# A two-layer fp32 encoder: output projection of the scan mixer requested one block ahead, a mask scaling moved from VectorE to ScalarE, and a shorter Newton step

## The chip, the cores and the metric

The kernel runs on one core of a Trainium2 chip. The metric is device time in microseconds (us) for one launch, median of three runs. The engines of a core each have their own instruction queue and run in order: TensorE (PE, with its weight loads PEld), VectorE (DVE), ScalarE (ACT), GpSimd (POOL), and SyncE (SP), which here issues the DMA transfers.

## The reference, cut to what matters

```
x: (1, 512, 1024) float32
layer 0:  h = rms_norm(x) @ w_in
          (A) neighbourhood attention, 8 heads of 64
          (B) Mamba-2 scan, 16 heads in 4 groups, 4 chunks of 128 tokens, forward and backward:
              y_diag = sum_s cb[l,s] * exp(a_cum[l] - a_cum[s]) (s <= l) * dt[s] x[s]
              y_off  = C . state . exp(a_cum);  gated by silu(z), group RMS norm
          x = x + concat(A, B) @ w_out          # "output projection", 1536 -> 1024
          x = x + swiglu_ffn(x)
layer 1:  GQA attention with QK norm and axial rotary; x = x + ctx @ w_out;  x = x + swiglu_ffn(x)
```

Every matrix product is fp32-accurate. The kernel splits each operand into a high part `h` and a low part `l` and makes three matmuls of each product (`l.h`, `h.l`, `h.h`).

## The kernel before, in words

All activations lie transposed: eight tiles `res[k]` of 128 channels by 512 tokens. A weight block of 1024 columns is loaded by `load_w` (L139 to L156): one DMA brings the raw block (tag `wr`, two buffers), ACT copies it to the high part (L147, tag `wh`, three buffers), DVE subtracts to get the low part (L149, tag `wl`, three buffers). Eight `mm3` calls, 24 matmuls 512 columns wide, use it. `stream(blocks, ahead)` (L166) takes a list of pairs (a function that loads, a generator that makes the matmuls) and calls the load of block n+1 before the matmuls of block n.

The mixer of layer 0 uses such a stream as filler. The generator `fill` yields after each `mm3`; `run(n)` takes n steps of it between the pieces of the attention and of the scan. PE's order is fixed by hand there (`manual_schedule` for PE); the order on DVE, ACT, POOL and SP is made by a planner, which goes by the order in which the instructions are written and by when it believes their inputs to be ready. The filler has 64 steps of query and key blocks, 192 steps of the scan's input blocks (four groups of six blocks of eight), and then the output projection, `out_blocks` (L696), which stands outside the stream: each of its blocks requests its weights and then at once makes its matmuls. It takes the eight output tiles in three trios; in each trio there are three blocks `oA` of eight steps on the first eight input tiles, and then one block `wq` of six (four in the last trio) on the two tiles of scan group 2. Group 3's two tiles come last, in `tail`.

The last input block of group 3 ends at step 256. The scan of group g starts at step 64 + 48(g+1) + LEAD[g] and takes 10, 8, 10, 2 and 12 steps of filler between its pieces; that of group 2 starts after step 220, so step 256 falls into its last 12 steps, six of which are then steps of the first `oA` block. Behind these stand, on PE, the matmuls `yd` (L650) and `yo` (L663) of group 2's second pair of heads, and then the transposes `bt` (L560) with which group 3 begins. They read the tile `grp` of group 3, on which ACT makes one silu (L542), with a load of its function table ahead of it. The silu needs the convolution of the last input block: one ACT instruction (L522) and three on DVE (L525).

For each of the 16 scan heads, lanes with tag `n` (eight buffers, 128x512) hold `m` (the masked `cb` times `dt`), `cf` and `cb` (two broadcast rows, by DMA), and for heads of a group's second pair (`i == 1`) also `mb`. The forward half of `m` is made by ACT in four chunks (L632). The backward half is added by DVE in four chunks (L634) for the first pair, and by one POOL instruction (L626) and one DVE addition (L641) for the second. The decay `cf` goes through ACT (L636), DVE or POOL (L638, L628, L643), an Exp on ACT (L644) and a product with `m` on DVE (L645), which PE needs for `yd`.

An inverse root is refined by one Newton step: three DVE operations on 128x512 (L205 to L207, L1042 to L1044; 16 times in all) or on a few columns (L214 to L216).

Layer 1 begins with `odd_mixer`. Two key blocks, `kpa` and `kpb`, are made by `project` (L173), and the sum of squares of `res` is made by seven POOL additions (L191) on squares from ACT, while the last blocks of the feed-forward before it are still running. In this mixer the planner orders PE too.

Of the kernel before, what the change touches and what calls it, by code (L numbers as in the profile page):

```python
# [11 lines left out]
AF = mybir.ActivationFunctionType  # L12
ALU = mybir.AluOpType
# [4 lines left out]
P = 128  # L18
# [54 lines left out]
def encoder_kernel(ctx: ExitStack, tc: tile.TileContext, xt, vec, cst, rope, nab, w_v, w_qk, w_dt, w_ssd,  # L73
# [98 lines left out]

    def project(ps, src, xg, name, eng=None):  # L173
        w = load_w(src, 1024, name, eng)
        for k in range(KB):
            mm3(ps, w, k * P, xg[k], ALL, k == 0, k == KB - 1)

# [16 lines left out]
    def rsqrt_wide(ps, inv, name):  # L194
        m = slot(f"{name}_m")
        A.activation(m, ps, AF.Identity, scale=inv, bias=epst)
        return rsqrt_tile(m, name)

    def rsqrt_tile(m, name):
        r = slot(f"{name}_r")  # L200
        t = slot(f"{name}_t")
        A.activation(r, m, AF.Ln)
        A.activation(r, r, AF.Exp, scale=-0.5)
        A.activation(t, r, AF.Square)
        V.tensor_tensor(t, t, m, ALU.mult)  # L205
        V.tensor_scalar(t, t, -0.5, 1.5, ALU.mult, ALU.add)
        V.tensor_tensor(r, r, t, ALU.mult)  # L207
        return r

    def rsqrt_small(m, r, t):  # L210
        A.activation(r, m, AF.Ln)
        A.activation(r, r, AF.Exp, scale=-0.5)
        V.tensor_tensor(t, r, r, ALU.mult)
        V.tensor_tensor(t, t, m, ALU.mult)  # L214
        V.tensor_scalar(t, t, -0.5, 1.5, ALU.mult, ALU.add)
        V.tensor_tensor(r, r, t, ALU.mult)  # L216

# [7 lines left out]
    def even_mixer(lp):  # L225
# [330 lines left out]
        def ssd_group(g, gt):  # L556
# [52 lines left out]
            for i in range(2):  # L609
                yd = bank(f"yd{g}_{i}", "c")  # L610
                es = []
                for hh in range(2):
# [8 lines left out]
                    def per_chunk(t):  # L621
                        return t[:, :, 16 + h:17 + h].to_broadcast([P, NCH, P])

                    if mm:
                        mb = lane(f"mb{h}", "n", 8)
                        G.tensor_tensor(c4(mb), c4(cbg), per_chunk(d3v(dt)), ALU.mult)  # L626
                    if em:
                        G.tensor_tensor(c4(cbk), c4(cbk), per_chunk(d3v(cum)), ALU.subtract)  # L628
                    for c in range(NCH):
                        cc = slice(c * P, (c + 1) * P)  # L630
                        jf, jb = c * 32 + h, c * 32 + 16 + h
                        A.activation(m[:, cc], cbl[:, cc], AF.Copy, scale=dt[:, jf:jf + 1])  # L632
                        if not mm:
                            V.scalar_tensor_tensor(m[:, cc], cbg[:, cc], dt[:, jb:jb + 1], m[:, cc],  # L634
                                                   ALU.mult, ALU.add)
                        A.activation(e[:, cc], cf[:, cc], AF.Identity, bias=ncum[:, jf:jf + 1])  # L636
                        if not em:
                            V.scalar_tensor_tensor(e[:, cc], cbk[:, cc], cum[:, jb:jb + 1], e[:, cc],  # L638
                                                   ALU.subtract, ALU.min)
                    if mm:  # L640
                        V.tensor_tensor(m, m, mb, ALU.add)  # L641
                    if em:
# [53 lines left out]
        def out_blocks():  # L696
            for trio in (range(3), range(3, 6), range(6, KB)):
                ps = {}
                for o in trio:
                    ps[o] = bank(f"oA{o}")  # L700
                    w = load_w(w_o0[o, :, 0:8 * P], 8 * P, f"wo{o}", V)
                    for k in range(8):
                        mm3(ps[o], w, k * P, (ctx_n + ssd_out)[k], ALL, k == 0, False)
                        yield
                w = load_w([w_o0[o, :, 8 * P:10 * P] for o in trio], 256 * len(trio), f"wq{trio[0]}", V)
                for n, o in enumerate(trio):
                    res[o] = xslot(f"xr{o}")
                    nc.sync.dma_start(res[o], xt[o])
                    for k in range(2):
                        mm3(ps[o], w, (2 * n + k) * P, ssd_out[4 + k], ALL, False, k == 1)  # L710
                        yield
                    V.tensor_tensor(res[o], res[o], ps[o], ALU.add)

        blocks = [t for b in range(4) for t in qk_blocks(b)] + [t for g in range(SSD_G) for t in ssd_blocks(g)]

        def both():
            yield from stream(blocks, 1)
            yield from out_blocks()

        fill = both()  # L720
        steps, later = [0], []

# [57 lines left out]
    def ffn(layer, gname, hp):  # L780
# [232 lines left out]
        with tc.manual_schedule(engines={mybir.EngineType.PE, mybir.EngineType.DVE, mybir.EngineType.Activation}):  # L1013
# [19 lines left out]
            def norm():  # L1033
                ps = bank(f"{name}_ss", "c")
                T.matmul(ps, ones_r, ql, start=True, stop=False)
                T.matmul(ps, ones_r, qh, start=False, stop=True)
                m, r, t = (slot(f"{name}_{n}") for n in "mrt")
                A.activation(m, ps, AF.Identity, scale=1.0 / D, bias=epst)
                A.activation(r, m, AF.Ln)
                A.activation(r, r, AF.Exp, scale=-0.5)  # L1040
                A.activation(t, r, AF.Square)
                V.tensor_tensor(t, t, m, ALU.mult)  # L1042
                V.tensor_scalar(t, t, -0.5, 1.5, ALU.mult, ALU.add)
                V.tensor_tensor(r, r, t, ALU.mult)  # L1044
                rstd.append(r)
# [77 lines left out]
    def odd_mixer(op):  # L1123
# [39 lines left out]
        pa, pb = bank("kpa"), bank("kpb")  # L1163
        project(pa, w_kv[0], xg, "wka")
        project(pb, w_kv[1], xg, "wkb")
        acc = sumsq("o")
        ksq = [slot(f"oksq{n}") for n in range(2)]
# [358 lines left out]
```

## Time and profile before

| | us |
|---|---|
| three runs | 1288.01, 1289.76, 1290.24 |
| median | 1289.76 |
| the profiled execution: its time | 1290.49 |
| its span, first to last instruction | 1288.7 |
| around the span | 1.8 |
| mean granted TensorE clock | 0.995 |

The profile is of one execution, 0.73 us above the median of the three runs. Times inside it are counted from the span's start. The layers lie in it so: attention and scan of layer 0 from 0 to about 350, feed-forward to about 718, layer 1's attention to about 925, feed-forward to the end. An instruction's row gives its start and its duration; a figure in square brackets is how long its engine stood idle before it and what released it.

### The profile page before, as it was taken

What the parts mean: (1) busy time and instruction counts of PE and PEld (TensorE: products, weight loads), DVE (VectorE), ACT (ScalarE), POOL (GpSimd) and SP (SyncE); (2) the same over time, 40 slices, a digit from 0 to 9 for tenths busy, and PEclk for the clock granted to TensorE, in tenths of its full rate; (3) what the DMA queues carried; (4) which work ended last, traced back from release to release, by engine and by line L of the source; (5) the groups of instructions that cost most, each with busy time, mean ns of one, the idle gap of its engine ahead of it and who ended that gap; (6) DMA issues with size and microseconds to landing.
All of it is one profiled execution on the core that took longest, in us unless ns stands there. A gap on an engine that the chain in (4) does not pass through costs nothing.

```text
span 1288.7 us, 20006 instructions
## 1 busy us (share of the span) xinstructions
PE 1264.0 (98%) x7502; PEld 1101.0 (85%) x7502; DVE 1000.4 (78%) x1688; ACT 716.1 (56%) x1335; POOL 166.4 (13%) x184
## 2 busy tenths in 40 slices
PE   9999999989999999999999999999999999999998
PEld 8777788867888899989998778778888899889987
DVE  6788798997789898738953668998889998549732
ACT  6676568766455456514643547777565455325521
POOL 5022111011100000000002334655100000000000
PEclk9999999999999999999999999999999999999999
DMA  7334343545333333332223443321223333423132
GB/s 235 107 99 148 112 138 123 164 120 166 123 116 113 99 99 114 117 98 84 91 78 96 144 97 101 83 66 34 83 82 98 106 107 104 123 79 105 54 117 92
DMA packets 52081, 139.03 MB, mean 108 GB/s; under 512 B 6992, under 2 KB 8144, under 8 KB 51984
## 3 DMA queue, kind: packets, MB, share of 16 engines
q1 hardware_dynamic: 51696, 137.23, 34.7%
q8 instruction: 59, 0.97, 0.3%
q10 hardware_dynamic: 288, 0.52, 0.1%
q14 instruction: 38, 0.31, 0.1%
HBM read 127.11 MB, written 2.23 MB: 100 GB/s over the span
## 4 chain that ended last, share of the span: by engine, by line
PE 70%; DVE 17%; ACT 6%; issue 4%; DMA 2%; SPq 0%; POOL 0%; ACTq 0%; DVEq 0%; POOLq 0%
PE fo L160 5%; PE fo L162 5%; PE fo L161 5%; PE fa L162 5%; PE fa L161 5%; PE fa L160 5%; PE fb L161 3%; PE fb L160 3%; PE fb L162 3%; PE vps L278 2%; PE opt L1281 1%; PE fc L162 1%; PE fc L161 1%; PE fc L160 1%; PE fg L1009 1%
## 5 line engine op out<-in xcount | busy, mean ns | idle before, releaser
L147 ACT ACTIVATE wf_h<-wf_r 128x1024 fp32r<-128x1024 f32 (+1 forms) x76 | 69.5, 919 | 125.8 <-PE fo L162 68.3
L160 PE MATMUL fo<-hh,wf_l 128*128 128x512 f32 x352 | 137.2, 390 | 1.2 <-DVE wf_l L149 1.2
L161 PE MATMUL fo<-hl,wf_h 128*128 128x512 f32 x352 | 137.0, 389 | 0.0
L162 PE MATMUL fo<-hh,wf_h 128*128 128x512 f32 x352 | 136.9, 389 | 0.0
L984 DVE TENSOR_TENSOR xr<-xr,fo 128x512 f32<-128x512 f32 x48 | 32.2, 685 | 113.6 <-PE fo L162 113.6
L149 DVE TENSOR_TENSOR wf_l<-wf_r,wf_h 128x1024 fp32r<-128x1024 f32 (+1 forms) x76 | 78.8, 1053 | 15.0 <-ACT wf_h L147 15.0
L160 PEld LDWEIGHTS fo<-hh,wf_l 128*128 128x128 f32 x352 | 66.1, 188 | 15.5 <-DVE wf_l L149 2.0
L162 PEld LDWEIGHTS fo<-hh,wf_h 128*128 128x128 f32 x352 | 66.1, 188 | 13.8
L161 PEld LDWEIGHTS fo<-hl,wf_h 128*128 128x128 f32 x352 | 66.1, 188 | 13.6
L160 PE MATMUL g<-n_xh,w_l 128*128 128x512 f32 x192 | 76.6, 399 | 0.0
L162 PE MATMUL g<-n_xh,w_h 128*128 128x512 f32 x192 | 75.3, 392 | 0.0
L161 PE MATMUL g<-n_xl,w_h 128*128 128x512 f32 x192 | 75.2, 392 | 0.0
L910 ACT ACTIVATE sl<-sb 128x256 f32<-128x256 f32 x34 | 14.3, 419 | 90.7 <-DVE sb L909 90.7
L191 POOL TENSOR_TENSOR o_acc<-o_acc,o_sq 128x512 f32<-128x512 f32 x7 | 12.3, 1753 | 383.2 <-ACT o_sq L190 383.2
L1272 POOL TENSOR_SCALAR op<-op,osum 128x512 f32<-128x512 f32 x64 | 45.4, 718 | 55.5 <-DVE osum L1271 38.6
L1270 ACT ACTIVATE op<-os,omx 128x512 f32<-128x512 f32 x64 | 43.6, 686 | 15.1 <-DVE omx L1268 12.9
L1285 DVE TENSOR_TENSOR opt<-opt,opt 128x512 fp32r<-128x512 f32 x64 | 43.5, 683 | 7.2 <-ACT opt L1284 6.5
L1284 ACT ACTIVATE opt<-opt 128x512 fp32r<-128x512 f32 x64 | 37.9, 598 | 18.7 <-PE opt L1281 18.1
L791 ACT ACTIVATE sa<-fa 128x256 f32<-128x256 f32 x68 | 25.4, 374 | 36.3 <-PE fa L162 36.3
L1268 DVE TENSOR_REDUCE omx<-os 128x1 f32<-128x512 f32 x64 | 42.0, 679 | 4.5 <-PE os L1266 4.4
L791 ACT ACTIVATE gh<-gr 128x1024 fp32r<-128x1024 f32 x34 | 35.6, 1047 | 14.0 <-PE fo L162 11.6
L162 PEld LDWEIGHTS g<-n_xh,w_h 128*128 128x128 f32 x192 | 36.1, 188 | 7.5
(2644 smaller groups left out, 4363.9 us busy)
## 6 DMA issues: line engine op xcount, KB each, us to landing
ur<-in_w_fa SPq DMA_DIRECT2D x34, 512.0 KB, 3.6
gr<-in_w_fa SPq DMA_DIRECT2D x34, 512.0 KB, 3.5
w_r<-in_w_ssd SPq DMA_DIRECT2D x24, 512.0 KB, 3.7
wf_r<-in_w_fa SPq DMA_DIRECT2D x20, 512.0 KB, 3.6
wf_r<-in_w_fb SPq DMA_DIRECT2D x32, 320.0 KB, 3.0
wf_r<-in_w_fb SPq DMA_DIRECT2D x16, 512.0 KB, 3.5
wo_r<-in_w_o SPq DMA_DIRECT2D x14, 512.0 KB, 3.8
nb<-in_nab SPq DMA_DIRECT2D x16, 256.0 KB, 3.0
```

The source lines that it names most:

```text
L147: A.activation(hi[:, 0:cols], raw, AF.Copy)
L149: (eng or V).tensor_tensor(lo[:, 0:cols], raw, f(hi)[:, 0:cols], ALU.subtract)
L160: T.matmul(ps, wl[:, a], xh[:, b], start=first, stop=False, skip_group_check=skip)
L161: T.matmul(ps, wh[:, a], xl[:, b], start=False, stop=False, skip_group_check=skip)
L162: T.matmul(ps, wh[:, a], xh[:, b], start=False, stop=last, skip_group_check=skip)
L791: A.activation(dst, src, AF.Copy, scale=scale)
L984: V.tensor_tensor(res[o], res[o], self.banks[o], ALU.add)
L1268: V.tensor_reduce(mx, sps, AX.X, ALU.max, negate=True)
L1270: A.activation(p_, sps, AF.Exp, bias=mx, accum_out=sums)
L1272: G.tensor_scalar(p_, p_, sums, 1.0, ALU.mult, ALU.mult)
L1284: A.activation(hl[:, 0:S], pt, AF.Copy)
L1285: V.tensor_tensor(hl[:, S:2 * S], pt, f(hl[:, 0:S]), ALU.subtract)
```

## The change

- `out_blocks` becomes a list of pairs like the others and is appended to `blocks`, so the stream requests each of its weight blocks one block ahead; `both` goes away. The order of the matmuls stays.
- For heads of a group's first pair, the backward half of the mask is scaled by four ACT copies into a lane `mb` of its own, and one DVE addition (that of the second pair) joins the halves. Four DVE operations per head go away.
- `newton` does the step in two `scalar_tensor_tensor` operations: t = (t * -0.5) * m, r = (t + 1.5) * r.
- `project` gets an order for `kpa` in which the eight matmuls with the low part of the activations come last.
- The sum of squares of layer 1's attention is added on DVE (`V`) and no longer on POOL.

```
-    def project(ps, src, xg, name, eng=None):
-        w = load_w(src, 1024, name, eng)
-        for k in range(KB):
-            mm3(ps, w, k * P, xg[k], ALL, k == 0, k == KB - 1)
+    def project(ps, src, xg, name, late=False):
+        wh, wl = load_w(src, 1024, name)
+        order = [(k, p) for k in range(KB) for p in range(3)]
+        if late:
+            order = [(k, p) for k in range(KB) for p in (0, 2)] + [(k, 1) for k in range(KB)]
+        for m, (k, p) in enumerate(order):
+            T.matmul(ps, (wl if p == 0 else wh)[:, k * P:k * P + P], xg[k][p == 1], start=m == 0, stop=m == 23)
...
+    def newton(r, t, m):
+        V.scalar_tensor_tensor(t, t, -0.5, m, ALU.mult, ALU.mult)
+        V.scalar_tensor_tensor(r, t, 1.5, r, ALU.add, ALU.mult)
...
-        V.tensor_tensor(t, t, m, ALU.mult)
-        V.tensor_scalar(t, t, -0.5, 1.5, ALU.mult, ALU.add)
-        V.tensor_tensor(r, r, t, ALU.mult)
+        newton(r, t, m)
...
+                    mb = lane(f"mb{h}", "n", 8)
                     if mm:
-                        mb = lane(f"mb{h}", "n", 8)
                         G.tensor_tensor(c4(mb), c4(cbg), per_chunk(d3v(dt)), ALU.mult)
...
                         A.activation(m[:, cc], cbl[:, cc], AF.Copy, scale=dt[:, jf:jf + 1])
                         if not mm:
-                            V.scalar_tensor_tensor(m[:, cc], cbg[:, cc], dt[:, jb:jb + 1], m[:, cc],
-                                                   ALU.mult, ALU.add)
+                            A.activation(mb[:, cc], cbg[:, cc], AF.Copy, scale=dt[:, jb:jb + 1])
...
-                    if mm:
-                        V.tensor_tensor(m, m, mb, ALU.add)
+                    V.tensor_tensor(m, m, mb, ALU.add)
...
         def out_blocks():
-            for trio in (range(3), range(3, 6), range(6, KB)):
-                ps = {}
-                for o in trio:
+            ps = {}
+
+            def first(o):
+                def matmuls(w):
                     ps[o] = bank(f"oA{o}")
-                    w = load_w(w_o0[o, :, 0:8 * P], 8 * P, f"wo{o}", V)
                     for k in range(8):
                         mm3(ps[o], w, k * P, (ctx_n + ssd_out)[k], ALL, k == 0, False)
                         yield
...
+                return (lambda: load_w(w_o0[o, :, 0:8 * P], 8 * P, f"wo{o}", V)), matmuls
...
+            for trio in (range(3), range(3, 6), range(6, KB)):
+                for o in trio:
+                    yield first(o)
+                yield rest(trio)
...
-        def both():
-            yield from stream(blocks, 1)
-            yield from out_blocks()
-
-        fill = both()
+        blocks += out_blocks()
+        fill = stream(blocks, 1)
...
-        project(pa, w_kv[0], xg, "wka")
+        project(pa, w_kv[0], xg, "wka", True)
         project(pb, w_kv[1], xg, "wkb")
-        acc = sumsq("o")
+        acc = sumsq("o", V)
```

## Rows read from the trace of the kernel before

**Rows 1.** The page's list of engines: busy us, share of the span, number of instructions.

```profile
PE 1264.0 (98%) x7502; PEld 1101.0 (85%) x7502; DVE 1000.4 (78%) x1688; ACT 716.1 (56%) x1335; POOL 166.4 (13%) x184
```

**Rows 2.** Busy time by stretch of 40 us: the scan of group 2, the stretch in which the output projection begins, and one of layer 1's attention. Columns: stretch, its length, then busy us (instructions) of PE, PEld, DVE, ACT and POOL, granted clock, DMA share, GB/s.

```profile
240.00:280.00 40.00, 39.20 (x226) 32.68 (x225) 37.81 (x66) 31.36 (x60) 4.46 (x4) 1.00 0.42 130
280.00:320.00 40.00, 33.57 (x168) 26.49 (x167) 31.70 (x56) 26.44 (x49) 3.63 (x2) 0.91 0.52 162
840.00:880.00 40.00, 37.51 (x215) 31.25 (x214) 37.11 (x71) 28.87 (x62) 21.52 (x22) 0.96 0.20 54
```

**Rows 3.** The waits of PE over the whole span, longest in total first: who waited, for what, us in total, times, longest.

```profile
PE oA L160 <- ACT cf L636: 4.6, 1, 4.6
...
PE oq_ss L1185 <- DVE oqsq L1235: 1.3, 1, 1.3
...
PE yd L650 <- DVE cf L645: 1.1, 2, 0.8
...
PE oA L160 <- ACT so_xh L180: 0.6, 1, 0.6
PE oA L161 <- DVE so_xl L181: 0.6, 2, 0.3
...
PE kpa L161 <- DVE o_xl L181: 0.5, 1, 0.5
```

**Rows 4.** PE in order of time, from the last matmul of the last scan input block to the first transpose of group 3.

```profile
280.93 0.39 PE L162 MATMUL g<-n_xh,w_h 128*128 128x512 f32 x1
285.91 0.76 PE L160 MATMUL oA<-nch,wo_l 128*128 128x512 f32 x1 [4.60 <-ACT cf L636]
...
292.92 1.09 PE L650 MATMUL yd<-cf,xtok 128*64 128x128 f32 x16
...
295.62 0.63 PE L560 MATMUL bt<-cstt,grp 128*128 128x128 f32 x4
```

**Rows 5.** Busy time of PE in the idle stretch and in the stretch behind it. Columns: stretch, length, PE busy (matmuls), granted clock, DMA share, GB/s.

```profile
281.40:285.90 4.50, 0.00 (x0) 0.89 0.59 117
285.90:291.90 6.00, 5.99 (x14) 0.51 0.51 154
```

**Rows 6.** DVE in order of time over the same place.

```profile
283.89 0.74 DVE L525 SCALAR_TENSOR_TENSOR grp<-g,vect,grp 128x510 f32<-128x510 f32 x1
284.55 1.21 DVE L149 TENSOR_TENSOR wo_l<-wo_r,wo_h 128x1024 fp32r<-128x1024 f32 x1
285.69 0.68 DVE L645 TENSOR_TENSOR cf<-cf,m 128x512 f32<-128x512 f32 x1
286.29 0.74 DVE L525 SCALAR_TENSOR_TENSOR grp<-g,vect,grp 128x511 f32<-128x511 f32 x1
286.95 1.21 DVE L149 TENSOR_TENSOR wo_l<-wo_r,wo_h 128x1024 fp32r<-128x1024 f32 x1
288.08 0.74 DVE L525 SCALAR_TENSOR_TENSOR grp<-g,vect,grp 128x511 f32<-128x511 f32 x1
```

**Rows 7.** ACT in order of time over the same place and the 15 us ahead of it.

```profile
267.35 1.05 ACT L147 ACTIVATE wo_h<-wo_r 128x1024 fp32r<-128x1024 f32 x1
269.44 1.28 ACT L632 ACTIVATE m<-cbl,dt 128x128 f32<-128x128 f32 x4 [1.03 <-DVE cf L645]
...
276.73 1.04 ACT L147 ACTIVATE wo_h<-wo_r 128x1024 fp32r<-128x1024 f32 x1
281.36 0.78 ACT L522 ACTIVATE grp<-g,vect 128x512 f32<-128x512 f32 x1 [3.58 <-PE g L162]
...
288.90 1.28 ACT L542 ACT_TABLE_LOAD   x1 [3.03 <-DVE grp L525]
290.19 2.77 ACT L542 ACTIVATE grp<-grp 128x3072 f32<-128x3072 f32 x1
```

**Rows 8.** ACT in order of time just ahead of the first `wq` block of the output projection.

```profile
313.48 0.41 ACT L636 ACTIVATE cf<-cf,ncum 128x128 f32<-128x128 f32 x1 [2.86 <-DMA cf<-cumd]
...
314.38 0.71 ACT L180 ACTIVATE so_xh<-yn,vect 128x512 fp32r<-128x512 f32 x1
```

**Rows 9.** Groups of instructions by line and operation over the whole span: line, engine, operation, output from inputs, shapes, count, then busy us, mean ns of one, and idle us before them with what ended it.

```profile
L632 ACT ACTIVATE m<-cbl,dt 128x128 f32<-128x128 f32 x64 | 22.7, 393 | 2.7 <-DVE cf L645 1.5 <-DVE cbl L577 1.2
L636 ACT ACTIVATE cf<-cf,ncum 128x128 f32<-128x128 f32 x64 | 22.2, 392 | 12.4 <-DMA cf<-cumd 12.4
L634 DVE SCALAR_TENSOR_TENSOR m<-cbg,dt,m 128x128 f32<-128x128 f32 x32 | 11.0, 395 | 0.0
L641 DVE TENSOR_TENSOR m<-m,mb 128x512 f32<-128x512 f32 x8 | 5.8, 740 | 0.0
L205 DVE TENSOR_TENSOR kn_t<-kn_t,kn_m 128x512 f32<-128x512 f32 x4 | 2.8, 690 | 1.8 <-ACT kn_t L204 1.8
L206 DVE TENSOR_SCALAR kn_t<-kn_t 128x512 f32<-128x512 f32 x4 | 1.7, 419 | 0.0
L181 DVE SCALAR_TENSOR_TENSOR f_xl<-xr,vect,f_xh 128x512 fp32r<-128x512 f32 x16 | 11.1, 745 | 0.0
L191 POOL TENSOR_TENSOR o_acc<-o_acc,o_sq 128x512 f32<-128x512 f32 x7 | 12.3, 1753 | 383.2 <-ACT o_sq L190 383.2
```

**Rows 10.** DVE in order of time while `kpa` is made.

```profile
721.23 2.44 DVE L181 SCALAR_TENSOR_TENSOR o_xl<-xr,vect,o_xh 128x512 fp32r<-128x512 f32 x2
```

More of the change, by code (lines that the diff above doesn't have):

```diff
@@ L213, in rsqrt_small @@
         V.tensor_tensor(t, r, r, ALU.mult)
-        V.tensor_tensor(t, t, m, ALU.mult)
-        V.tensor_scalar(t, t, -0.5, 1.5, ALU.mult, ALU.add)
-        V.tensor_tensor(r, r, t, ALU.mult)
+        newton(r, t, m)
     def bcast_rstd(acc, name):
@@ L704, in out_blocks, with rest, matmuls @@
                         yield
[L705 to L712, printed above, removed]
+                return (lambda: load_w(w_o0[o, :, 0:8 * P], 8 * P, f"wo{o}", V)), matmuls
+            def rest(trio):
+                def matmuls(w):
+                    for n, o in enumerate(trio):
+                        res[o] = xslot(f"xr{o}")
+                        nc.sync.dma_start(res[o], xt[o])
+                        for k in range(2):
+                            mm3(ps[o], w, (2 * n + k) * P, ssd_out[4 + k], ALL, False, k == 1)
+                            yield
+                        V.tensor_tensor(res[o], res[o], ps[o], ALU.add)
+                return (lambda: load_w([w_o0[o, :, 8 * P:10 * P] for o in trio], 256 * len(trio),
+                                       f"wq{trio[0]}", V)), matmuls
+            for trio in (range(3), range(3, 6), range(6, KB)):
+                for o in trio:
+                    yield first(o)
+                yield rest(trio)
         blocks = [t for b in range(4) for t in qk_blocks(b)] + [t for g in range(SSD_G) for t in ssd_blocks(g)]
-        def both():
-            yield from stream(blocks, 1)
-            yield from out_blocks()
-        fill = both()
+        blocks += out_blocks()
+        fill = stream(blocks, 1)
         steps, later = [0], []
@@ L1041, in norm @@
                 A.activation(t, r, AF.Square)
-                V.tensor_tensor(t, t, m, ALU.mult)
-                V.tensor_scalar(t, t, -0.5, 1.5, ALU.mult, ALU.add)
-                V.tensor_tensor(r, r, t, ALU.mult)
+                newton(r, t, m)
                 rstd.append(r)
```

## The prediction, made before the change was run

> **What bounds the kernel now.** I read the list of engines first, then the stretches of 40 us, then PE's waits, and last the order of time on PE, DVE and ACT at the one large wait. The list shows PE busy for 98% of the span [rows 1]: no change to the other engines can be worth more than the time in which PE waits or runs slowly, and the reader should look for that time only. The change takes no matmul away. The stretches show where such time lies: 40 us pass with PE busy for 33.6 and a mean granted clock of 0.91 where the output projection begins, and in the scan ahead of it PE is full while DVE is busy for 37.8 of 40 and ACT for 31.4; layer 1's attention loses some 2.5 us in a like stretch [rows 2]. PE's waits name the largest, 4.6 us ahead of the first `oA` matmul [rows 3].
>
> The order of time tells what that wait is. The profile puts it down to ACT `cf`, whose data these matmuls do not read. What they read are the weights: the high part was copied at 276.7 at the latest, in fact both copies of `wo` then made were over by 277.8 [rows 7], but DVE made the low part only from 284.55 to 285.76, and PE began at 285.91 [rows 4, 6]. So the data lay ready for 7 us or more, and the low part stood behind other work on DVE, because the load is written late in the program. The idle time has a second price: in the 6.0 us behind it the granted clock was 0.51, that is the level of 1.2 GHz [rows 5]. At full clock that work would have taken 6.0 x 0.51 = 3.1, so 2.9 us are lost. The last matmul ahead started at 280.93 and PE was free some 0.25 later, at 281.2; the first `oA` came at 285.91, 4.7 us later. The place costs 4.7 + 2.9 = 7.6 us.
>
> **The change part by part.**
>
> *One block ahead.* The load of the first `oA` block is now written ahead of the last input block of group 3, before the elementwise work of group 2's second pair of heads, so DVE should make its low part before 281.2. Then the 18 matmuls ahead of `yd` follow at once: 285.91 to 292.92 less the 2.9 lost is 4.1 us. `yd` and `yo` take 295.62 - 292.92 = 2.7 [rows 4]. PE would stand before `bt` at 281.2 + 4.1 + 2.7 = 288.0, where it came at 295.62 before.
>
> But `bt` reads the silu of group 3, which ended at 290.19 + 2.77 = 292.96 [rows 7]. This is what is late next. Its chain starts when PE ends the last input block: ACT at 281.36, three DVE operations at 283.89, 286.29 and 288.08, the table load at 288.90, the silu. Between the three stand two weight parts of 1.21 [rows 6]. One of them, the first `wo`, leaves this place; the next starts 285.69 - 284.55 = 1.14 us later than it could, so the silu ends at about 291.8 if the rest keeps its order. PE then waits 291.8 - 288.0 = 3.8 us at `bt`. The gain up to `bt` is 295.6 - 291.9 = 3.7 us. If the clock falls behind this wait as it fell behind the one of 4.6, another 2.9 are lost and 0.8 stays; if not, 3.7. The best end is a chain without foreign work on DVE: 281.36 + 0.78 + 3 x 0.74 + 1.28 + 2.77 = 288.4 [rows 6, 7], and 7.2 us gained. Between 0.8 and 3.7 I take 2.2, as no row shows which way a wait between the two goes. DVE's 1.2 us for the low part do not vanish; they fall earlier, where DVE is full [rows 2], and are covered as long as `yd` finds `cf` ready: it did at 286.4, when L645 ended [rows 6], and PE would come at 285.3. Up to 1.1 us of wait at `yd` is therefore inside the 3.8, not on top of it.
>
> *The wait for `so`.* Further on, the first `wq` block waits for group 2's output, `so`: 0.6 + 0.6 = 1.2 us [rows 3]. ACT made `so_xh` at 314.38, behind a `cf` instruction that had waited 2.86 for its DMA [rows 8]. With group 3 running some us earlier on all engines, DMA and norm move against each other. Bounds: 0 and 1.2; I take 0.6.
>
> *Second mask scaling on ACT.* DVE loses 32 chunk operations, 11.0 us busy, and gains eight additions, 5.8; ACT gains 32 copies like those of L632, 1.28 for four, 10.2 us in all [rows 7, 9]. Over four groups that is -1.3 us of DVE and +2.6 us of ACT in a stretch of about 40, against 37.8 and 31.4 busy [rows 2]: ACT comes to 34 and stays below DVE. What is hidden: the ACT copies run ahead of `cf`, in ACT's idle time (12.4 us of it before `cf`, waiting for DMA [rows 9]). What may show: PE's two waits at `yd` for DVE, 1.1 us in total [rows 3]; the addition is shorter than the chunks were. Bounds: +1.1 gained, and a loss if the copies delay Exp; I take 0.5 gained. If the cover were gone, 10.2 us of ACT would stand in the chain to `yd`.
>
> The Trainium skill (ScalarE: Activation LUTs, Rules for kernel authors) says that additions and multiplications belong on VectorE and not on ScalarE, which speaks against this edit. The trace does not bear it out for this shape: the copy took 393 ns on ACT and the fused operation 395 ns on DVE [rows 9]. By the rule the edit would cost more on ACT than DVE saves; by the rows the two are equal per chunk, and only the load of the engines decides.
>
> *Newton.* Three operations, 0.690 + 0.419 + 0.690 = 1.80, become two of the kind that took 0.745, 1.49 [rows 9]: 0.31 x 16 = 5.0 us of DVE. Most lie under matmuls: around the norms of the feed-forward PE does not wait [rows 3]. Five of the sixteen are in layer 1's attention, where PE loses time to DVE [rows 2, 3]: at most 5 x 0.31 = 1.6 us. I take 0.3. The small forms save one operation each and show nowhere.
>
> *Low part last, and the sum on DVE.* `kpa` waited 0.5 us for `o_xl`, in a stretch where two such operations took 2.44 instead of 2 x 0.745 [rows 3, 9, 10]. With 16 matmuls ahead of the first low part, the wait goes: 0.5 gained (bounds 0 and 0.5). The seven additions, 12.3 us on POOL, become 7 x 0.690 = 4.8 on DVE [rows 9], five or six of them under the last feed-forward blocks, where DVE has idle time; they cost nothing while that lasts, and 0.7 each if one falls between the last `o_xl`.
>
> *Sum:* 2.2 + 0.6 + 0.5 + 0.3 + 0.5 = 4.1 us. The profiled execution would go from 1290.49 to 1286.4; it lay 0.7 above the median, so against 1289.76 I forecast **1285.6**. All best ends give 7.2 + 1.2 + 1.1 + 1.6 + 0.5 = 11.6, or 1278.2; the bounds without a new mechanism end at 1289.0 (0.8 and nothing else).
>
> **The rivals.** A measurement of this kernel tells about 0.2% (2.6 us) from no change.
>
> *Handed on whole.* The wait moves from `oA` to `bt`, the clock falls there again, and `so` and `yd` wait as before: 1289.76 - 0.8 - 0.5 = 1288.5, not to be told from no change. For it speaks that the silu's chain hangs on PE's own last input block and on a full DVE [rows 2, 6], and that the planner puts a ready weight part into any gap, the second `wo` too. Against it: one of two weight parts does leave the chain.
>
> *Silu close behind.* The planner makes the three convolution operations nearly in a row; PE waits 0.5 to 2 us at `bt` and the clock stays up: 6 to 7 us there and 2 elsewhere, about 1281. For it speaks that less DVE work stands there; against it that the planner's order was wrong here before.
>
> *Lanes short (the slower side).* Eight lanes held three heads' tiles at three each; two heads now fill all eight. Already ACT's `m` waited 1.03 us for the release of a lane by L645 [rows 7]. The third head's `cf` cannot be requested until a lane returns, and it then waits for its DMA, with the rest of ACT's queue (Exp, `so_xh`, weight copies) behind it, and PE's `yd` and `wq` behind those. The worst such wait was 2.86 [rows 8]; one in each of four groups is 11.4 us, less 4.1 gained: 1297. It decides from about 1.7 us per group on, when it exceeds the gain by what can be measured. Against it: the second pair is needed some 12 filler steps after the first, and the lanes of `cb` and `mb` return early.
>
> **How the numbers follow.** The likeliest case, partly handed on, 1283.5 to 1287.2: 0.40. Silu close behind: 0.18. Handed on whole: 0.28. Lanes short, or another order of the planner's that costs as much: 0.14. So faster 0.58, same 0.28, slower 0.14. The range, 1280.0 to 1291.5, leaves out the tail of the best ends and most of the slower case.
>
> **What would show it.** In the profile after: no wait of PE for the first `oA`, which starts within 0.3 us of the last `g`; `wo_l` on DVE before that; a new wait at `bt` for ACT `grp` (L542) of 2 to 4 us, and a clock near 0.5 or 1.0 behind it, which decides between the first two cases. L634 gone, 32 more ACT copies, 16 additions `m`; no 12.3 us on POOL; no wait of `kpa`. The prediction is wrong if `bt` does not wait at all, if `yd` waits over 1.7 us in each group, or if layer 1's attention, where the planner also orders PE, moves by more than 2 us either way.

## The result, and the profile after

The changed kernel takes 1281.24 us (median of five runs, 1279.26 to 1281.94), the kernel before, on the same chip at the same time, 1288.95 (1288.01 to 1290.24). The ratio is 0.9933 with a 95% interval of 0.992 to 0.9947: 7 to 10 us less. I had forecast 1285.6, with a range of 1280.0 to 1291.5. The direction is right, the time lies inside the range, and the gain is about twice the forecast. The profiled execution of after took 1281.94, its span is 1280.2.

The page's list of engines, which answers to [rows 1]:

```profile
PE 1258.6 (98%) x7502; PEld 1100.6 (86%) x7502; DVE 990.8 (77%) x1649; ACT 723.9 (57%) x1367; POOL 154.4 (12%) x177
```

DVE lost 9.6 us and 39 instructions, ACT gained 7.8 us and 32 instructions, POOL lost 12.0. PE has the same matmuls as before. So the gain is again time in which PE waited or ran slowly, and the waits of PE tell more than the busy times do. Over the whole span of after they are (longest first; who waited, for what, us in total, times, longest), to be held against [rows 3]:

```profile
PE bt L563 <- ACT grp L545: 4.0, 1, 4.0
PE os L1273 <- ACT op L1278: 2.7, 1, 2.7
PE oq_ss L1193 <- DVE oqsq L1243: 2.4, 1, 2.4
PE kss L362 <- ACT ksq L360: 1.4, 1, 1.4
...
PE yd L651 <- DVE cf L646: 0.8, 1, 0.8
```

The wait of 4.6 us at `oA` is gone, and so are those for `so_xh`, `so_xl` and `kpa`. A wait of 4.0 us at `bt` is new. In layer 1's attention those at `os` and `oq_ss` have grown, from 1.5 and 1.3. PE in order of time at this place, which answers to [rows 4]:

```profile
278.67 0.39 PE L162 MATMUL g<-n_xh,w_h 128*128 128x512 f32 x1
278.90 0.39 PE L160 MATMUL oA<-nch,wo_l 128*128 128x512 f32 x1
...
283.07 1.40 PE L651 MATMUL yd<-cf,xtok 128*64 128x128 f32 x16
284.40 1.60 PE L664 MATMUL yo<-grp,H 128*128 128x128 f32 x12
289.97 1.11 PE L563 MATMUL bt<-cstt,grp 128*128 128x128 f32 x4 [3.96 <-ACT grp L545]
```

The first `oA` follows the last `g` after 0.23 us, the pitch of two matmuls in a row, and `yd` and `yo` follow without a wait. Then PE stands. DVE's and ACT's order there, which answers to [rows 6] and [rows 7]:

```profile
271.50 1.21 DVE L149 TENSOR_TENSOR wo_l<-wo_r,wo_h 128x1024 fp32r<-128x1024 f32 x1
...
281.99 0.74 DVE L528 SCALAR_TENSOR_TENSOR grp<-g,vect,grp 128x510 f32<-128x510 f32 x1
...
283.25 0.75 DVE L528 SCALAR_TENSOR_TENSOR grp<-g,vect,grp 128x511 f32<-128x511 f32 x1
283.91 1.22 DVE L149 TENSOR_TENSOR wo_l<-wo_r,wo_h 128x1024 fp32r<-128x1024 f32 x1
285.04 0.74 DVE L528 SCALAR_TENSOR_TENSOR grp<-g,vect,grp 128x511 f32<-128x511 f32 x1
```

```profile
285.86 1.28 ACT L545 ACT_TABLE_LOAD   x1 [1.57 <-DVE grp L528]
287.15 2.76 ACT L545 ACTIVATE grp<-grp 128x3072 f32<-128x3072 f32 x1
```

The first low part is ready at 272.71, 6.2 us before PE needs it. One low part still stands between the three convolution operations, where there were two. The silu ends at 289.91, and `bt` starts 0.06 later. The clock at this place, which answers to [rows 5] (stretch, length, PE busy with its matmuls, granted clock, DMA share, GB/s):

```profile
278.90:283.00 4.10, 4.10 (x19) 1.00 0.48 136
...
289.90:296.00 6.10, 6.03 (x31) 0.76 0.96 225
```

Ahead of the wait the clock stays at its full level, 2.4 GHz. Behind it the mean is 0.76, so that part of the stretch ran at 1.2 GHz, and 6.1 x 0.24 = 1.5 us are lost.

**Where the gain lies in time.** For each matmul that two traces have in common I took its start in both. The table gives the median difference (us, the named kernel less before) over matmuls that began in the named ten us of the trace of before. One execution of each kernel stands behind it. In the four kernels with 18 or 24 steps of filler (e6, e10, e11, e12) PE's order differs from that of before between 290 and 360; a matmul that was only moved would pass there for time gained, so these cells stay empty.

| kernel | 130 | 170 | 270 | 300 | 340 | 700 | 730 | 900 | end |
|---|---|---|---|---|---|---|---|---|---|
| after | -1.8 | -1.7 | -2.3 | -5.3 | -7.0 | -7.5 | -8.4 | -8.2 | -8.5 |
| e1_ahead | 0.0 | 0.1 | 0.5 | -0.9 | -0.6 | -0.5 | -0.6 | 0.3 | 0.3 |
| e2_newton | -3.3 | -3.2 | -1.8 | -2.1 | -3.7 | -4.2 | -4.2 | -4.9 | -5.3 |
| e3_mask | 0.1 | 0.1 | -1.1 | -2.2 | -4.1 | -4.1 | -4.2 | -3.0 | -2.6 |
| e4_odd | 0.5 | 0.6 | 1.4 | 1.3 | 1.1 | 1.1 | 0.3 | 1.5 | 1.5 |
| e5_no_ahead | -3.3 | -3.3 | -3.8 | -4.5 | -6.2 | -6.6 | -7.5 | -7.2 | -7.6 |
| e6_quota18 | -2.6 | -2.6 | -3.1 | – | – | -10.3 | -11.2 | -10.9 | -11.3 |
| e7_newton_wide | -2.9 | 5.1 | 6.3 | 5.2 | 3.5 | 3.1 | 3.1 | 0.9 | 0.5 |
| e8_newton_spare | -2.0 | 4.9 | 5.3 | 5.0 | 4.4 | 3.9 | 3.9 | 2.8 | 2.8 |
| e9_wide_pin | -2.7 | -1.0 | 0.2 | -1.0 | -2.4 | -2.8 | -2.8 | -2.4 | -2.7 |
| e10_q18_pool | -2.8 | -2.8 | -3.4 | – | – | -9.1 | -10.0 | -11.3 | -11.5 |
| e11_q18_no_ahead | -3.1 | -3.1 | -3.4 | – | – | -6.6 | -7.5 | -8.8 | -9.2 |
| e12_q24 | -2.9 | -2.9 | -3.1 | – | – | 7.2 | 6.4 | 4.6 | 4.3 |

In e4_odd every queue up to 600 us holds the same instructions in the same order as before, and still its starts lie up to 1.4 later. The changed kernel and e5_no_ahead have the same order up to 250, and lie 1.8 and 3.3 ahead at 130; e6_quota18 and e10_q18_pool have the same order up to 600, and lie 10.3 and 9.1 ahead at 700. A difference of up to some 1.5 us may thus be chance in one execution; what several kernels with the same edit repeat between the same two columns, and waits that appear or vanish by name, are not.

Read across, the row of after says: 1.7 to 1.8 gained before 130, in the attention of layer 0; 3.0 from 270 to 300, where `oA` and `bt` lie; 1.7 up to 340, where the waits for `so` stood (1.6 to 1.9 in e2, e3 and e5 too); 0.9 at `kpa` (0.8 to 0.9 wherever that edit is in). Only the second of these is the place on which more than half of my forecast rested.

### The profile page after: what moved, and what is told of

It reads as the page before. It is cut to its first block, busy times and chain, and to the rows that moved or that the text cites. A ratio compares the mean times of both kernels' runs of the same rounds, so it can differ in the third digit from the quotient of the medians.

```text
span 1280.2 us, 19995 instructions
## 1 busy us (share of the span) xinstructions
PE 1258.6 (98%) x7502; PEld 1100.6 (86%) x7502; DVE 990.8 (77%) x1649; ACT 723.9 (57%) x1367; POOL 154.4 (12%) x177
## 4 chain that ended last, share of the span: by engine, by line
PE 71%; DVE 14%; ACT 7%; issue 4%; DMA 2%; POOL 0%; SPq 0%; DVEq 0%; ACTq 0%; POOLq 0%
PE fo L160 5%; PE fo L161 5%; PE fo L162 5%; PE fa L162 5%; PE fa L161 5%; PE fa L160 5%; PE fb L162 3%; PE fb L161 3%; PE fb L160 3%; PE opt L1289 2%; PE g L160 2%; PE g L161 2%; PE g L162 2%; PE vps L281 2%; PE fc L162 1%
## 5 line engine op out<-in xcount | busy, mean ns | idle before, releaser
L1349 POOL TENSOR_TENSOR wgvl<-wgv_r,wgvh 128x512 fp32r<-128x512 f32 x4 | 6.5, 1635 | 402.2 <-ACT wgvh L1348 400.3
L161 PEld LDWEIGHTS g<-n_xl,w_h 128*128 128x128 f32 x192 | 36.1, 188 | 7.4 <-DVE n_xl L184 0.8
```

The lines of the kernel that those rows point to most:

```text
L161: T.matmul(ps, wh[:, a], xl[:, b], start=False, stop=False, skip_group_check=skip)
```

## The experiments

Each verdict is the ratio to the kernel before on the same chip, with its 95% interval.

**The early request: alone, left out, and with more cover.** e1_ahead makes this edit and no other.

```
...
-            yield from stream(blocks, 1)
-            yield from out_blocks()
...
+        blocks += out_blocks()
+        fill = stream(blocks, 1)
```

> The kernel before with one part of the change: the output projection's weight blocks requested one block ahead. Theory (the request alone moves the wait to the silu and brings the rest of group 3 forward): the 4.6 us wait of the first oA goes, bt waits 3 to 4.5 us for the silu, some 1.5 us of clock are lost behind it, the waits for so (1.2 us) shrink or go; 3 to 5 us faster, about 1285. Rival (DVE time freed by the other edits is needed for it): the low part of the weights still comes late or the silu later than in the changed kernel, under 1.5 us gained, about 1288.

1289.85 us, ratio 0.9998 (0.9986 to 1.0009): nothing. DVE in order of time, the silu on ACT, and PE's largest wait:

```profile
280.05 1.21 DVE L149 TENSOR_TENSOR wo_l<-wo_r,wo_h 128x1024 fp32r<-128x1024 f32 x1
...
284.64 0.74 DVE L525 SCALAR_TENSOR_TENSOR grp<-g,vect,grp 128x510 f32<-128x510 f32 x1
285.30 1.21 DVE L149 TENSOR_TENSOR wo_l<-wo_r,wo_h 128x1024 fp32r<-128x1024 f32 x1
...
287.12 0.74 DVE L525 SCALAR_TENSOR_TENSOR grp<-g,vect,grp 128x511 f32<-128x511 f32 x1
287.78 1.21 DVE L149 TENSOR_TENSOR wo_l<-wo_r,wo_h 128x1024 fp32r<-128x1024 f32 x1
288.92 0.74 DVE L525 SCALAR_TENSOR_TENSOR grp<-g,vect,grp 128x511 f32<-128x511 f32 x1
```

```profile
291.31 2.76 ACT L542 ACTIVATE grp<-grp 128x3072 f32<-128x3072 f32 x1
```

```profile
PE bt L560 <- ACT grp L542: 4.2, 1, 4.2
```

The first low part did leave the chain of the convolution, but the third, requested earlier too, took its place: two still stand between the three operations, as before. The silu ends 12.6 us after the start of PE's last `g` (at 281.49 here), where it took 12.0 in before. The rival "handed on whole" is what this edit does by itself.

e5_no_ahead is the changed kernel with these lines as they were before.

> The changed kernel with the output projection's weights requested late again, as before; the other four edits stay. Alone, the early request gained nothing that could be measured. Theory (the early request is worth its 3 us up to bt only together with the mask edit, which frees DVE ahead of it): this kernel has the 4.6 us wait at the first oA and is 3 to 4 us slower than the changed one, about 1285. Rival (the edits add up, and the early request is worth nothing here too): within 1.5 us of the changed kernel, about 1281.

1281.24 us, ratio 0.9942 (0.9929 to 0.9954), against 0.9933 with the edit: the request brings less than can be told there, and the rival came true. PE waits 3.8 us at `oA` again. One wait of about 4 us stands in place of another, and in these two executions that is not quite even: from 270 to 300 after gains 3.0 and e5_no_ahead 0.7.

```profile
277.15 0.39 PE L162 MATMUL g<-n_xh,w_h 128*128 128x512 f32 x1
281.29 0.77 PE L160 MATMUL oA<-nch,wo_l 128*128 128x512 f32 x1 [3.75 <-ACT cf L638]
```

```profile
285.57 2.77 ACT L545 ACTIVATE grp<-grp 128x3072 f32<-128x3072 f32 x1
```

Here the silu ends 11.2 us after the start of the last `g`, as in after (278.67 to 289.91), though two low parts stand in this chain and one in after's. So the chain is 0.8 shorter than in before by the other edits, and not by the request; e2_newton and e3_mask alone leave it at 12.0.

If so, the request should pay as soon as PE has work while the silu is made. e6_quota18 gives it that: six more steps of filler between the last pieces of group 2, the 18 matmuls of six `mm3`, ahead of `yd` and `yo`.

```
-SSD_QUOTA = (..., (10, 8, 10, 2, 12), (10, 8, 10, 2, 12))
+SSD_QUOTA = (..., (10, 8, 10, 2, 18), (10, 8, 10, 2, 12))
```

> The changed kernel with 18 filler steps in place of 12 ahead of the second yd of group 2, so that six more mm3 (4.1 us) of the output projection stand ahead of bt. Theory (bt waits for the silu only because nothing else stands there for PE): the 4.0 us wait shrinks to under 1 us, no clock is lost behind it, and the whole is 3 to 5 us faster than the changed kernel, about 1277. Rival (the scan of group 3 behind it, on DVE and ACT, is the limit, so that later steps wait instead, for H, so or yd): under 1 us gained.

1278.84 us (1278.32 to 1279.14), ratio 0.9917 (0.9905 to 0.993), some 2 us under the changed kernel, where I had expected 3 to 5; the intervals of the two ratios overlap. PE in order of time, and the clock there:

```profile
288.44 1.60 PE L664 MATMUL yo<-grp,H 128*128 128x128 f32 x12
290.12 0.63 PE L563 MATMUL bt<-cstt,grp 128*128 128x128 f32 x4
```

```profile
290.00:297.00 7.00, 6.59 (x39) 1.00 0.66 176
```

`bt` starts when it did in after, at 290.1, but 18 more matmuls lie ahead of it, PE does not wait, and the clock stays at 1.00. The 4.0 us of the wait and the 1.5 of the clock are gone. Of these 5.5, 2.8 are left from the feed-forward on (10.3 ahead at 700 against 7.5), and 0.8 of that e6_quota18 had already at 270, where its queues do not differ yet. Waits for `so_xl` (0.9), `so_xh` (0.7) and `wo_l` (0.8) have come back; what follows on PE now comes sooner, and the norm of group 2 does not.

e11_q18_no_ahead is the same with the late request.

> e6_quota18 with the output projection's weights requested late again. Theory, order only: with less VectorE work ahead the low part is made in time either way, as e5_no_ahead suggests; 1278 to 1280, no more than 1 us from e6_quota18. Rival, request needed: with 18 steps TensorE reaches the second and third oA block before group 3 begins, each of whose weights is then late; a wait of 3 us or more ahead of oA, 1281 to 1285.

1282.25 us (1280.91 to 1283.09), ratio 0.9938 (0.9926 to 0.995), as the rival had it; PE waits at `oA` again:

```profile
PE oA L160 <- DVE wo_l L149: 3.8, 1, 3.8
```

With cover at `bt` the early request is worth 3.4 us (against e10_q18_pool below, on the same chip, which differs besides in the engine of layer 1's sum and is as fast as e6_quota18). Without cover it is worth nothing that can be told: 0.9998 alone, 0.9933 against 0.9942 in the changed kernel, where the intervals leave room for some 3 us. The wait and what it is handed on to are two terms in series; the cover must be there for the request to show.

e12_q24 goes on, with 24 steps.

> The changed kernel with 24 instead of 12 steps of filler between the last pieces of scan group 2 (e6_quota18: 18). Theory, cover spent: with 18 no wait was left at bt, so more filler there buys nothing and moves group 3 later, nearer to the end of the filler; 1278.5 to 1281, and the waits for so grow by 1 us or more. Rival, still short of cover: silu's tail is still exposed as low clock or small waits; 1276 to 1278.

1294.54 us, ratio 1.0035 (1.0022 to 1.0048): slower than the kernel before. Its starts are 7.2 behind those of before at 700. Its largest waits:

```profile
PE oA L160 <- ACT so_xh L183: 8.0, 1, 8.0
PE t L160 <- ACT so_xh L183: 4.9, 1, 4.9
```

The filler is a stock. With 24 steps the `oA` steps that need nothing of group 2 are used up sooner: at 301.7 PE comes to `wq`, which reads group 2's output, and its norm ends only 8.0 us later. At the end `t` waits 4.9 for group 3's. Behind both waits the clock was at its lower level (0.51 from 309.7 to 316.4, 0.51 from 364.1 to 371.0). The sign was as expected; I had put the loss against e6_quota18 at 2 us at most, and it was 16.

**The Newton step.** e2_newton makes this edit alone (both the wide and the small forms).

```
...
-        V.tensor_tensor(t, t, m, ALU.mult)
-        V.tensor_scalar(t, t, -0.5, 1.5, ALU.mult, ALU.add)
-        V.tensor_tensor(r, r, t, ALU.mult)
+        V.scalar_tensor_tensor(t, t, -0.5, m, ALU.mult, ALU.mult)
+        V.scalar_tensor_tensor(r, t, 1.5, r, ALU.add, ALU.mult)
```

> The kernel before with one part: Newton steps in two operations. The changed kernel is already 1.7 us ahead of the kernel before at 130 us, ahead of any scan work. Theory (that lead is Newton's, through another order of the planner's in the attention of layer 0): PE is 1.5 to 2 us ahead at 130 us and about 2 us at the feed-forward, and the attention of layer 1 gives or takes up to 1 us; 1 to 3 us faster. Rival (Newton's operations are hidden, as the prediction's small term said, and the lead at 130 us comes from elsewhere): within 0.5 us at 130 us, and no change in the whole.

1285.05 us, ratio 0.9953 (0.994 to 0.9965), 4 to 8 us for an edit that I had put at 0.3 in the prediction and at 1 to 3 here. The table has 3.3 of it before 130. First the trace of before there, in rows that the prediction did not use: PE in order of time, and the window behind its wait.

```profile
79.75 0.50 PE L160 MATMUL kps<-early,wk_l 128*128 128x512 f32 x1 [1.90 <-DVE wk_l L149]
80.09 1.86 PE L359 MATMUL kss<-ksq,cstt 128*128 128x512 f32 x2
```

```profile
79.75:84.00 4.25, 4.25 (x13) 0.60 0.40 129
```

Then the same two views of e2_newton:

```profile
78.31 1.12 PE L359 MATMUL kss<-ksq,cstt 128*128 128x512 f32 x2 [1.41 <-ACT ksq L357]
...
79.51 0.40 PE L160 MATMUL kps<-early,wk_l 128*128 128x512 f32 x1
```

```profile
78.35:82.60 4.25, 4.25 (x19) 1.00 0.52 139
```

Before, PE waited 1.9 us for a low part that stood on DVE behind other work, and then ran 4.25 us at a mean clock of 0.60, which lost 4.25 x 0.40 = 1.7 us more: 3.6 in all. With two operations the low part starts at 77.09 instead of 78.48 and this wait is gone. Another of 1.4 takes its place, behind which the clock stays up. 3.6 - 1.4 = 2.2. In columns of five us the starts gain 2.4 between 70 and 85, and the same 2.4 in every kernel that has the short step in the wide forms and nothing added to it, the changed kernel too (2.4 to 2.5); 0.0 in e1, e3 and e4. The rest of the 3.3 is within chance: the changed kernel, with the same order of every queue up to 130, was 0.9 behind at 70.

The low part is not all that moved. PE's order is fixed by hand in the scan, but not, as I had written of the whole mixer, in the attention ahead of it: there the planner orders PE too. Before, the first `kps` stands ahead of `kss`; with the edit it stands behind it, with `nsc` between them. ACT's order differs from 35 us on, PE's from 40.

To learn which operations count, and whether it is their number in the chain or DVE's time, two more kernels: e7_newton_wide keeps three operations in the small forms (edit against e2_newton),

```
     def rsqrt_small(m, r, t):
...
-        newton(r, t, m)
+        V.tensor_tensor(t, t, m, ALU.mult)
+        V.tensor_scalar(t, t, -0.5, 1.5, ALU.mult, ALU.add)
+        V.tensor_tensor(r, r, t, ALU.mult)
```

> The kernel before with the two-operation Newton step only in the 128x512 forms; the forms on a few columns keep their three operations. Theory (the wide forms make the gain, since two turns in DVE's queue in place of three bring kr of the key blocks 1.2 us forward): 3 us ahead at 130 us and 4 to 5 us faster in the whole, as with all forms. Rival (the short chains of q, or just another order of the planner's, make it): under 2 us ahead at 130 us.

and e8_newton_spare adds to every step of e2_newton a third operation on which nothing depends.

```
...
+        V.tensor_scalar(spare[:, 0:m.shape[-1]], m, -0.5, 1.5, ALU.mult, ALU.add)
         V.scalar_tensor_tensor(t, t, -0.5, m, ALU.mult, ALU.mult)
```

> The kernel before with the two-operation Newton step everywhere, and beside it one more DVE operation that reads m and writes a spare tile that nobody reads, as long as the one taken away (0.42 us on 512 columns): DVE is as busy as before, but the chain has two steps. Theory (what counts is the number of dependent steps, each of which waits for its turn): still 3 us or more faster. Rival (what counts is DVE's time): within 1.5 us of the kernel before.

1292.65 us, ratio 1.0024 (1.0014 to 1.0034), and 1293.52, ratio 1.003 (1.0019 to 1.004): both are slower than the kernel before, and neither theory came true as a whole, nor did a rival. Both keep the lead at 130 (-2.9 and -2.0). In e7_newton_wide it is gained at the same place (2.4 between 70 and 85), so the wide forms alone make it. In e8_newton_spare it is 2.1 there, but in another way:

```profile
78.86 0.50 PE L160 MATMUL kps<-early,wk_l 128*128 128x512 f32 x1 [1.80 <-DVE wk_l L149]
```

```profile
78.86:83.10 4.24, 4.24 (x20) 1.00 0.62 157
```

With the third operation back, `kps` stands ahead of `kss` again and PE waits 1.8 us for the low part, as it did before; only the slow clock behind the wait is missing. So this kernel does not tell the shorter chain from the time saved on DVE, nor either from PE's order.

Both kernels then lose 7 to 8 us between 140 and 165. In e7_newton_wide, DVE's longest wait in this stretch, and ACT's order:

```profile
DVE wst L506 <- ACT wst L505: 4.7, 1, 4.7
```

```profile
144.18 1.28 ACT L544 ACT_TABLE_LOAD   x1 [2.94 <-DVE grp L527]
145.47 2.77 ACT L544 ACTIVATE grp<-grp 128x3072 f32<-128x3072 f32 x1
148.26 1.28 ACT L547 ACT_TABLE_LOAD   x1
149.56 0.31 ACT L505 ACTIVATE wst<-wst 128x128 f32<-128x128 f32 x1
```

The planner has put the silu of scan group 0 with its two table loads, 5.3 us, ahead of a short Exp on which DVE's next instruction hangs, and with it the tiles of the attention. In e8_newton_spare the silu stands ahead too; in before, e2_newton and after the Exp does. e9_wide_pin therefore is e7_newton_wide with the silu held behind that Exp and one copy.

```
...
-                    si = A.activation(gt, gt, AF.Silu)
+                    with tc.issue_after(pin[0]), tc.issue_after(nps5[0]):
+                        si = A.activation(gt, gt, AF.Silu)
```

> The kernel before with the two-operation step in the wide forms alone (as in e7_newton_wide), and with ScalarE's first silu (scan group 0) held behind the Exp of wst and the nps copy of head 5, as the planner puts it in e2_newton by itself; nothing is left out. Theory, order: what e7_newton_wide lost between 140 and 160 us is this one place in ScalarE's queue (silu and two table loads, 5.3 us, ahead of Exp wst). Then the VectorE product wst waits under 1 us instead of 4.7, the lead of about 2.9 us at 130 us is still there at 170, and the time is 1284 to 1287 instead of 1292.65. Rival, length: the small forms with three steps make the loss; then the lead is gone by 170 again and the time stays above 1290.

ACT's Exp, and the product on DVE that hangs on it:

```profile
144.64 0.31 ACT L510 ACTIVATE wst<-wst 128x128 f32<-128x128 f32 x1 [3.22 <-DVE wst L509]
```

```profile
145.28 0.27 DVE L511 TENSOR_TENSOR wst<-wst,dt 128x128 f32<-128x128 f32 x1
```

The product follows the Exp at once. 1287.86 us, ratio 0.9985 (0.9976 to 0.9995). From 130 to 170 it loses 1.7 where e7_newton_wide lost 8.0: this one place in one queue is worth 6.3 us. The median came out 1 us above the 1284 to 1287 of the theory and well below the rival's 1290. What is still missing to e2_newton, about 2.7 in the table, is 1.5 at 140, where PE waits 1.2 at `npt` for POOL, and some 1.3 near 740. Whether the small forms cause these, or again the order, these runs do not tell.

The pages of e2_newton and e7_newton_wide give DVE the same busy time, 8.4 us less than in before:

```profile
PE 1260.0 (98%) x7502; PEld 1099.4 (86%) x7502; DVE 992.0 (77%) x1666; ACT 715.0 (56%) x1335; POOL 170.3 (13%) x184
```

```profile
PE 1262.1 (98%) x7502; PEld 1100.0 (85%) x7502; DVE 992.0 (77%) x1672; ACT 715.4 (55%) x1335; POOL 166.6 (13%) x184
```

One gained 5.2 us, the other lost 2.8.

**The mask on ACT.** e3_mask makes this edit alone.

```
...
-                            V.scalar_tensor_tensor(m[:, cc], cbg[:, cc], dt[:, jb:jb + 1], m[:, cc],
-                                                   ALU.mult, ALU.add)
+                            A.activation(mb[:, cc], cbg[:, cc], AF.Copy, scale=dt[:, jb:jb + 1])
...
```

> The kernel before with one part: the second mask scaling on ScalarE. Theory: the yd wait of 0.8 us in group 2 goes or moves, DVE is 1.3 us less busy per group and ACT 2.6 us more, no lane wait shows; between 1.5 us faster and 0.5 us slower. Rival (lanes short): cf of the third head is requested only after the second head's product, yd of the second pair waits over 1.7 us in several groups; 4 to 8 us slower.

1286.7 us, ratio 0.9967 (0.9955 to 0.998): 3.5 us, more than the 1.5 that I had expected at best. The waits for `yd` (1.1) and `so` (1.2) of [rows 3] are both gone, and the starts at 340 are 4.1 earlier; 1.1 is given back by 900, where the wait for `oq_ss` is 2.1 instead of 1.3. Some 1 us of the 4.1 is the clock behind the wait at `oA`, which is 4.6 us long as before, and this may be chance; the granted clock there, against 0.51 in [rows 5]:

```profile
284.88:290.88 6.00, 6.00 (x20) 0.72 0.51 153
```

No wait of PE for a lane came up.

**Layer 1.** e4_odd makes the two edits there and no other.

```
-        project(pa, w_kv[0], xg, "wka")
+        project(pa, w_kv[0], xg, "wka", True)
...
-        acc = sumsq("o")
+        acc = sumsq("o", V)
```

> The kernel before with the two edits at the head of layer 1's attention: low part of the activations last in kpa, and the sum of squares on VectorE. Theory: PE is 0.7 to 0.9 us ahead after kpa and keeps some of it; 0.3 to 1 us faster in the whole, which is not to be told from no change. Rival: the attention, bound by DVE, takes it back within 50 us; 0 in the whole.

1289.44 us, ratio 0.9992 (0.9982 to 1.0001). The wait of `kpa` is gone, 0.8 from 700 to 730, and 1.2 are lost again by 900: the wait for `oq_ss` is 2.3 instead of 1.3. (The execution behind the table was the slowest of twelve, 2.6 above the median.) I took the sum on DVE for the cause, and e10_q18_pool puts it back on POOL in the fastest kernel.

```
-        acc = sumsq("o", V)
+        acc = sumsq("o")
```

> e6_quota18 with the sum of squares of layer 1's attention on GpSimd again. Theory, turns: on VectorE the seven additions stand in the queue ahead of the work for oq_ss; on GpSimd they do not, the wait for oq_ss falls by about 1 us, and the time is about 1278, 0.5 to 1.5 less than e6_quota18. Rival, slow adder: GpSimd's 12.3 us end after the last residual tile and the key norm waits for them; 1279 to 1281.

1278.87 us (1277.14 to 1279.29), ratio 0.991 (0.9897 to 0.9924), the same time as e6_quota18, where I had expected 0.5 to 1.5 less. The wait stayed:

```profile
PE oq_ss L1193 <- DVE oqsq L1243: 2.4, 1, 2.4
```

So the sum on DVE is not its cause, and no difference between the engines can be told. It is 2.4 in e9_wide_pin too, which has neither edit of layer 1, and 1.6 in e2_newton. What sets it stays open.

Alone, the four parts took 0.4, 5.2, 3.5 and 0.8 us off the median of before, 9.9 together; the whole change took off 7.7. They are not independent: the waits for `so` go with Newton alone and with the mask alone, and can be gained only once. (Those for `yd` go with the mask; with Newton alone they are 2.1.)

## Why the prediction was right, and where its sum was off

*What bounds the kernel, and the mechanism at `oA`: right.* The low part's place in DVE's queue was the cause; with the early request the wait went, and the silu's chain was late next, as worked out. I had said a wait of 3.8 us at `bt`, and 4.0 was measured; `oA` follows `g` in 0.23; `yd` does not wait there. The clock decided between the first two cases and came out between them, 1.5 us lost where I had 2.9 or nothing. The net at this place is 3.0 (from -2.3 to -5.3) against 2.2. One step was right in size by luck: I let the silu end 1.14 earlier because one low part leaves its chain. The chain did become 0.8 shorter, but without the request as well (e5_no_ahead, with two low parts in it), and with the request alone it became 0.6 longer (e1_ahead). DVE's other work takes the place of the low part that leaves; which of it decides stays open. So the credit isn't the request's alone: by itself it brought nothing.

*Newton: the term that failed.* The step of the prediction was "Most lie under matmuls", and a price of 0.3 by DVE's busy time and by what of it PE could see; the edit alone took 5.2 off. Busy time is the wrong measure: e2_newton and e7_newton_wide save the same 8.4 us of DVE (I had 5.0), and one is 5.2 faster, the other 2.8 slower. What moved is the order of the queues. In the attention of layer 0 it took away a wait and the slow clock behind it, 2.4 us; one silu ahead of one short Exp cost 6.3. That the small forms "show nowhere" was wrong in this way too: they alone lie between e2_newton and e7_newton_wide. Whether the chain of two operations, the time saved or PE's order made the first of these is not shown. I had also left the wait of 1.9 at `kps` out of the rows, though it was the second in PE's list, larger than any that I used but `oA`. It should have been a term, with bounds of 0 and 1.9 + 1.7 = 3.6.

*Mask: 0.5 taken, 3.5 measured alone.* The working of the cover was right: no wait of PE for ACT's copies came up with 32 more of them, and the waits at `yd` fell from 1.1 to 0.8 in after and to nothing in e3_mask. I gave the edit half of the `yd` wait alone and counted the `so` wait under the request. e3_mask has neither wait. The price per operation was right as well, in after's groups (busy us, mean ns of one, idle before):

```profile
L637 ACT ACTIVATE mb<-cbg,dt 128x128 f32<-128x128 f32 x32 | 12.3, 391 | 0.0
L642 DVE TENSOR_TENSOR m<-m,mb 128x512 f32<-128x512 f32 x16 | 12.1, 764 | 0.0
```

The Trainium skill (ScalarE: Activation LUTs, Rules for kernel authors) would have such a multiplication on VectorE, and gives the reason for bf16. For this fp32 shape the measurement decides: a copy took 391 ns on ACT, the fused operation on DVE, which also made the addition, 395 [rows 9], and the addition left on DVE 764 for four chunks. The engines' work grew, and e3_mask was 3.5 us faster, with DVE the fuller engine [rows 2].

*The wait for `so`: 0.6 taken, 1.7 gained.* All of it went, past my upper bound of 1.2; what the 0.5 above the waits is stays open. The condition I named, that DMA and norm move against each other, did not arise: ACT's `cf` no longer waited just ahead of `so_xh`.

*`kpa` and the sum: 0.5 taken, 0.9 at the place,* and nothing of it kept in e4_odd. That the seven additions cost nothing on DVE was right.

*The rivals.* Handed on whole (0.28) is true of the request alone and false of the whole. Silu close behind (0.18) had the right time, 1281, by luck and for a wrong reason: it needed a wait of 0.5 to 2 us and had 4.0. Lanes short (0.14) did not occur. But its second half, "another order of the planner's that costs as much", did: in e7_newton_wide and e8_newton_spare, on a small edit, with a price of 7 to 8 us at the place. The changed kernel escaped it.

*My signs of a wrong prediction:* `bt` does wait, `yd` does not wait over 1.7 in any group, layer 1's attention moves by under 2 us. None came up. So the mechanism held and the sum was half of the gain, by the terms of Newton (0.3 for 2.4 in after, between 70 and 85) and of `so` and the mask (1.1 for some 2.3, from 170 to 270 and from 300 to 340).

## What to carry to other kernels

Where a planner sets the order, the busy time that an edit saves on a full engine tells neither the size nor the sign of its gain: compare the order of every queue before and after, that of the bounding engine too, since a small edit can move a long instruction ahead of a short one for 6 us. Take every wait of the bounding engine into the sum, the ones far from the edit too, each with the slow clock behind it as a range and not as a number. A wait that is handed on pays only when the next one has cover: 18 steps of filler made the early request worth 3.4 us, with 12 it could not be told from nothing, and 24 ran out of stock and lost 16.

## What the hardware showed that I had not expected

The clock behind a wait: granted 0.51 over 6.0 us behind 4.6 us of waiting [rows 5], 0.76 over 6.1 us behind 4.0, 0.60 over 4.25 us behind 1.9, and 1.00 behind 1.4. The shortest of the three expensive waits lost nearly its own length again, 1.7 us; I had priced only the longest one for it. But the length of the wait alone does not set the loss: behind 4.6 us it was also 0.72 over 6.0 (e3_mask), behind 1.8 it was 1.00 (e8_newton_spare), and behind the 2.4 us at `oq_ss` it was one thing in after and another in e10_q18_pool:

```profile
740.45:744.00 3.55, 3.55 (x12) 0.58 0.61 134
```

```profile
738.92:742.50 3.58, 3.58 (x23) 1.00 0.67 147
```

What decides it these runs do not show. It is 1 to 2 us that the same wait may cost or not, and executions with the same queues differed by up to some 1.5 us in the first 300 us, so that a shift of this size in one trace is no evidence.
